# Three reorderings in a one-core diffusion layer: a gathered row inside the gate step, softmax normalising ahead of rotations, one engine per PSUM tile

## The chip, the cores and the metric

The kernel runs on one core of one Trainium2 chip. The metric is device microseconds (us) of one execution, here the median of three runs. One further execution was profiled; every view below comes from it. Engines are named as the profile names them: PE multiplies matrices, PEld loads its weights, DVE is the vector engine, ACT the scalar (activation) engine, POOL the general one, SP issues most transfers.

## The reference

One layer of a hybrid backbone over 512 latent tokens and 256 context tokens, width 1024. Modulated tokens go through one wide input projection into three branches: a gated linear recurrence, a convolution, and attention with 8 heads over 768 keys with a rotary position code. The branches are gated, summed, projected, and a first layer norm follows. Then come the product-key experts: each token picks 16 of 16384 single-neuron experts in each of 8 heads, and

    act = gelu(u_tab[expert] . t)        # 128 picked rows per token
    out = sum over k of (g * act)_k * v_tab[expert]_k

and a second layer norm.

## The kernel before, in words

The order of the work on PE, DVE, ACT and POOL is written out by hand: what stands first in the program goes first in that engine's queue. SP's transfers are not in that hand order; the framework plans them. All float32 products are made of three passes over a high part (ACT rounds, `whi`, `ph`, ...) and a low part (DVE subtracts the high part from the value, `wlo`, `pl`, ...): `mm3`, lines 142 to 144. So a low part always waits for ACT's high part.

**Attention** (`slot`, `norm`, `softmax`, `turn`) goes over 8 heads times 4 blocks of 128 queries. In slot n the kernel divides block n's exponentials by their sum (`norm`, L947 and L948), takes the row maximum of block n + 1 and starts its exponentials (`softmax`, L938 to L942), multiplies the scores of block n + 2 (`scores`), and transposes block n (`turn`: PE L956, then ACT and DVE split the result into `PTh` and `PTl`). Between these stand pieces of the next heads' projections, passed in as `early`, `mid` and `late`; among them the rotation of a query or key (`rope`, L831 to L833), whose first DVE operation waits for a PE product, and `fetch_next`, which splits the next weight block.

**Norm 1** (`project`, `normalise`, `turn1`, `modulate`, `parts1`) takes token blocks 1, 2, 3, 0. `turn1` transposes a normalised block into two PSUM tiles `pt` of four 128 x 128 pieces each; `modulate` scales and shifts the pieces into `tf`: for most blocks DVE takes the four of the first tile and ACT the four of the second; for block 3 DVE takes pieces 0 to 4 and ACT 5 to 7, so both read the second tile. `parts1` then splits `tf` into `xh` (ACT) and `xl` (DVE or POOL), which the first expert product `pu` reads.

**The expert loop.** Tokens 128 to 511 are not gathered: all 128 x 128 expert scores are computed densely. Pass i multiplies the gated activations of expert group i (`ph`, `pl`, 128 x 384) with 128 rows of the v table, `second`: 6 results, 18 matmuls of 512 columns into `acc`. Up to pass 69 the activations of group n = i + 1 were made earlier (they lie in `arun`, or come back from DRAM). From n = 71 on, pass i also makes them, `first`: 24 matmuls of 384 columns into `pa`. `weigh` multiplies the activations by the gates (L1602, DVE), and `halves` splits them: ACT makes `ph` (L137), DVE `pl` (L138). `ph` and `pl` have two buffers each, `wraw` (the landing place of weight blocks) three. The first 128 tokens are done by gathering: POOL fetches one row of the u or v table per token (L1478), 128 + 128 rows in all, into seven `raw` buffers, so up to six are asked for ahead; DVE multiplies each by the token and sums (L1489), or adds it to the running output (L1497). `shares` hands each pass its number of these `gather_step`s, about 1.18 up to pass 69 and 3.2 from there on (by the factors 1.1 and 3.0 in `budget`); they wait in the list `todo` and `some` takes them out between matmuls.

In DVE's queue a pass up to 69 therefore stands so: gate product, (ACT makes `ph`), `pl`, two `wlo`, one or two rows. From there on: two `wlo` of u, the rows, two `wlo` of v, gate product, (ACT makes `ph`), `pl`. In the last 32 passes `prepare` adds operations for the end: two small PE products, and in eight passes a DVE operation of 128 x 1024.

Of the kernel before, what the change touches and what calls it, by code (L numbers as in the profile page):

```python
# [9 lines left out]
F32 = mybir.dt.float32  # L10
# [7 lines left out]
AF = mybir.ActivationFunctionType  # L18
# [5 lines left out]
NB, NBC = T // 128, TC // 128  # L24
H = 8
# [69 lines left out]
def body(tc, I, O):  # L95
    nc = tc.nc
    V, A, P, G = nc.vector, nc.scalar, nc.tensor, nc.gpsimd
# [38 lines left out]
    def split(hi, lo, src):  # L136
        A.activation(hi, src, AF.Copy)  # L137
        V.tensor_sub(lo, src, hi.bitcast(F32))  # L138
# [12 lines left out]
    def pspow(out, ps, mul, tmp):  # L151

        V.tensor_scalar(tmp, ps, mul, EPS, op0=ALU.mult, op1=ALU.add)
        G.tensor_tensor(out, tmp, mhalf[:, :tmp.shape[-1]], op=ALU.pow)
# [79 lines left out]
    todo, ready = [], []  # L234
# [38 lines left out]
    for h in range(-1, H):  # L273
        n = h + 1
# [46 lines left out]
    def go(*gens):  # L321
        for g in gens:
            next(g, None)
# [94 lines left out]
    def query(h):  # L418
        x_ = hd[h]
        w = feed('in', Z_Q + h)  # L420
        ps = pmm.tile([128, T], F32, name="mm")
        yield from product(ps, w, xhl, 2)
        s = hp.tile([128, T], F32, name="sg")
        A.activation(s, ps, AF.Sigmoid)
        x_.q = hp.tile([128, T], F32, name="q", bufs=1)
        V.tensor_mul(x_.q, ps, s)
        yield
        x_.KM = hp.tile([128, T], F32, name="KM")
        V.tensor_add(x_.KM, x_.KS[:, 0, :], x_.KS[:, 1, :])
        x_.QP = hp.tile([128, 2, T], F32, name="QP")  # L430
        for d in range(2):
            V.tensor_mul(x_.QP[:, d, :], x_.q, x_.F[:, d, :])
        x_.tot = x_.F
        yield
# [128 lines left out]
    def norm():  # L563

        bc = pms.tile([128, T], F32, name="ms")
        P.matmul(bc, ones[:, 0:1].to_broadcast([128, 128]), usum, start=True, stop=True)
        qsum = hp.tile([128, T], F32, name="scT")
        last = None
        for j in range(KT):
            uj = u[:, j, :]  # L570
            V.scalar_tensor_tensor(uj, bc, -1.0 / D, uj, op0=ALU.mult, op1=ALU.add)
            sq = hp.tile([128, T], F32, name="KM")
            A.activation(sq, uj, AF.Square)
            if j:
                G.tensor_add(qsum, last, sq)
            last = qsum if j else sq
            if j % 3 == 2:
                yield
        yield
        st = pms.tile([128, NB], F32, name="ms")  # L580
        for b in range(NB):
            P.matmul(st[:, b:b + 1], qsum[:, b * 128:(b + 1) * 128], ones, start=True, stop=True)
        t1 = const.tile([128, NB], F32, name="lt")
        rs = const.tile([128, NB], F32, name="lrs")
        pspow(rs, st, 1.0 / D, t1)
        yield
        uhl.extend([mp.tile([128, KT, T], F32R, name="uhi"), hc.tile([128, KT, T], F32R, name="og")])
        bc = pst.tile([128, NB, 128], F32, name="bc")
        for b in range(NB):
            P.matmul(bc[:, b, :], rs[:, b:b + 1].to_broadcast([128, 128]), ident, start=True, stop=True)  # L590
        bc = bc[:].rearrange("p b t -> p (b t)")
        V.tensor_mul(u[:, 0, :], u[:, 0, :], bc)
        yield
        for j in range(KT):
            uj = u[:, j, :]
            if j + 1 < KT:
                V.tensor_mul(u[:, j + 1, :], u[:, j + 1, :], bc)
            s = mp.tile([128, T], F32, name="ms", bufs=2)
            A.activation(s, uj, AF.Sigmoid, scale=chan['clg'][:, j:j + 1], bias=chan['clb'][:, j:j + 1])
            V.tensor_scalar(uj, uj, chan['clg'][:, j:j + 1], chan['clb'][:, j:j + 1], op0=ALU.mult, op1=ALU.add)  # L600
            V.tensor_mul(uj, uj, s)
            A.activation(uhl[0][:, j, :], uj, AF.Copy)
            if j:
                V.tensor_sub(uhl[1][:, j - 1, :], u[:, j - 1, :], uhl[0][:, j - 1, :].bitcast(F32))
            yield
        V.tensor_sub(uhl[1][:, KT - 1, :], u[:, KT - 1, :], uhl[0][:, KT - 1, :].bitcast(F32))
        yield
# [48 lines left out]
    ip, f_, b_, q_ = inputs(0), direction(0, 0), direction(0, 1), query(0)  # L656
# [27 lines left out]
    for h in range(H):  # L684
        n = h + 1
# [7 lines left out]
        if n < H:  # L693
            ip, f_, b_, q_ = inputs(n), direction(n, 0), direction(n, 1), query(n)
# [70 lines left out]
    a_ = adas()  # L765
# [184 lines left out]
    def turn(b):  # L950
        p_ = pb.pop(b)[0]
        for q_ in range(2):
            pt = ppt.tile([128, 3, 128], F32, name="pt")
            for j in range(3):
                c = q_ * 3 + j
                P.transpose(pt[:, j, :], p_[:, c * 128:(c + 1) * 128], ident)  # L956
            o_ = [t_[:, q_ * 3:q_ * 3 + 3, b * 128:(b + 1) * 128] for t_ in PT]
            split(o_[0], o_[1], pt)
# [7 lines left out]
    def slot(n, early=(), late=(), mid=(), pre=()):  # L966

        h, b = divmod(n, NB)
        norm(h, b)
        if n + 1 < NB * H:  # L970
            softmax(*divmod(n + 1, NB))
        go(*pre)
        if n + 2 < NB * H:
            scores(*divmod(n + 2, NB))
        fetch_next()
        if b == 0 and h:
            out(h - 1)
        go(*early)
        fetch_next()
        go(*mid)  # L980
        turn(b)
        go(*late)
        fetch_next()

# [37 lines left out]
    for g in range(4):  # L1022
        n = 8 * g
# [139 lines left out]
    def modulate(b, pts):  # L1163
        tfs = []
        for q_, pt in enumerate(pts):
            tf = op.tile([128, 4, 128], F32, name="tf", bufs=4)
            for i in range(4):
                j = q_ * 4 + i
                if j > 4 if b == 3 else q_:
                    A.activation(tf[:, i, :], pt[:, i, :], AF.Identity, scale=gs[:, j:j + 1], bias=bs[:, j:j + 1])  # L1170
                else:
                    V.tensor_scalar(tf[:, i, :], pt[:, i, :], gs[:, j:j + 1], bs[:, j:j + 1], op0=ALU.mult, op1=ALU.add)
            tfs.append(tf)
        return tfs
# [70 lines left out]
    NA = 32  # L1245
# [9 lines left out]
    arun = gap.tile([128, NA, TD], F32, name="gt")  # L1255
# [335 lines left out]

    ph = {}

    def halves(i2, a_):
        names = ("raw", "raw") if i2 >= NT - 2 else ("ph", "pl")
        ph[i2] = [pp.tile([128, TD], F32R, name=n, bufs=RB[1] if n == "raw" else 2) for n in names]
        split(ph[i2][0], ph[i2][1], a_)

    def weigh(n, a_):

        v_ = a_.rearrange("p (b t) -> p b t", t=GB)
        V.tensor_tensor(v_, v_, gates[n // GN][:, :, n % GN, :], op=ALU.mult)  # L1602
        halves(n, a_)
        if n % GN == GN - 1:
            del gates[n // GN]
        read_gates(n)
# [16 lines left out]
    back = {}  # L1623
# [11 lines left out]
    todo = []  # L1635
# [6 lines left out]
    def first(n, left):  # L1642

        a_ = gap.tile([128, TD], F32, name="a", bufs=4)
        ps = pa.tile([128, TD], F32, name="pa")
        w = UV.pop(('u', n))
        for k in range(KT):
            mm3(ps, [t_[k // 4][:, k % 4, :] for t_ in w], [t_[:, k, :] for t_ in thd], k == 0, k == KT - 1)
            if k % 2:
                some(left - k // 2)  # L1650
        A.activation(a_, ps, AF.Gelu_apprx_tanh)
        return a_
# [69 lines left out]
    for i in range(NT - LAST):  # L1722
        n = i + 1
        todo += shares(i)
        left = 6
        if NU <= n:
            fetch(('u', n + 1))
            left = 10
            a_ = first(n, left)
        else:  # L1730
            if n + 1 == NU:
                fetch(('u', NU))
            if NA <= n + 1 < NU:
                back[n + 1] = gap.tile([128, TD], F32, name="a", bufs=4)
                nc.sync.dma_start(back[n + 1], ad[n + 1 - NA])
            weigh(n, arun[:, n, :] if n < NA else back.pop(n)[:])
        if ('v', n) not in UV:
            fetch(('v', n))
        for m in range(2):
            for b in range(NB - 1):  # L1740
                second(i, b, m)
                some(6 - 3 * m - b)
        if NU <= n:
            weigh(n, a_[:])
        if i >= NT - 32:
            prepare(i - NT + 32)
        if gathered[0] == 2 * NS_ and 0 not in nst:
            residual(0, 0)
            residual(0, 1)
            moments(0)  # L1750
            norm2(0, 0)
            norm2(0, 1)
        del UV['v', i], ph[i]
# [42 lines left out]
```

## Time and profile before

| | us |
|---|---|
| median of 3 runs | 2436.23 (2435.23 to 2440.38) |
| the profiled execution, its own time | 2440.56 |
| its span, first to last instruction | 2438.8 |
| PE busy | 2344.7 (96%) |
| DVE busy | 1935.6 (79%) |
| ACT busy | 1043.3 (43%) |
| POOL busy | 648.6 (27%) |
| mean granted TensorE clock | 0.99 of full speed |

Shares of busy time are means over stages: in some stages PE never stops, in others it waits for a low part. Attention runs from about 770 to 1037 us of the span, norm 1 until about 1155, the expert loop from 1603 to 2396.

### The profile page before, as it was taken

To read this page: it belongs to the slowest core of one execution; us is meant where nothing else is said; L and a number is where in the kernel's file an instruction comes from. 1 tells how busy PE (TensorE), PEld (TensorE's weight loads), DVE (VectorE), ACT (ScalarE), POOL (GpSimd) and SP (SyncE) were. 2 spreads that over 40 slices of the span, in tenths; PEclk is the share of its full clock that TensorE was granted. 3 is DMA by queue.
4 is the path that set the end of the run, shared out by engine and by line. 5 is a ranking of instruction groups with operands and counts; after the bars stand their busy time and mean duration, and the time that the engine had idled before them with its cause. 6 is when DMAs were issued, how large, how long until landed. Compare 5 with 4: busy or idle time off the path is not lost.

```text
span 2438.8 us, 34766 instructions
## 1 busy us (share of the span) xinstructions
PE 2344.7 (96%) x12547; PEld 2022.8 (83%) x12547; DVE 1935.6 (79%) x3736; ACT 1043.3 (43%) x2294; POOL 648.6 (27%) x555
## 2 busy tenths in 40 slices
PE   7999999999999999999999999999989999999997
PEld 3888888887887777877999999987767888898886
DVE  7788888887875566564999699968878788889886
ACT  5544444443423444643366645533333333332333
POOL 6000000002111000041688301122323344444432
PEclk9999999999999999999999999999999999999999
DMA  6211111111482111242323379999999989998962
GB/s 241 74 61 61 60 54 61 61 61 64 163 303 76 35 35 35 70 145 81 104 98 111 123 259 324 327 331 307 349 354 348 351 320 336 339 333 317 337 220 93
DMA packets 156973, 452.66 MB, mean 186 GB/s; under 512 B 16256, under 2 KB 60672, under 8 KB 154624
## 3 DMA queue, kind: packets, MB, share of 16 engines
q1 hardware_dynamic: 106976, 278.33, 32.9%
q0 software_dynamic: 36864, 134.23, 15.5%
q10 hardware_dynamic: 12960, 37.87, 4.1%
q8 instruction: 99, 1.62, 0.3%
q14 instruction: 74, 0.61, 0.1%
HBM read 411.77 MB, written 37.03 MB: 184 GB/s over the span
## 4 chain that ended last, share of the span: by engine, by line
PE 60%; DVE 24%; DMA 7%; ACT 5%; issue 3%; POOL 2%; ACTq 0%; DVEq 0%; POOLq 0%; SPq 0%
PE mm L142 13%; PE mm L144 13%; PE mm L143 13%; DVE wlo L131 6%; DVE raw L1489 4%; DMA wraw<-in_v_dram 3%; PE sc L455 2%; PE pg L1539 2%; ACT whi L129 2%; PE acc L142 2%; PE acc L143 2%; PE acc L144 2%; ACT ph L137 2%; DMA wraw<-in_uT_dram 2%; DVE ttok L1497 2%
## 5 line engine op out<-in xcount | busy, mean ns | idle before, releaser
L131 DVE TENSOR_TENSOR wlo<-wraw,whi 128x512 fp32r<-128x512 f32 x687 | 465.1, 719 | 156.3 <-ACT whi L129 155.0
L142 PE MATMUL mm<-xh,wlo 128*128 128x512 f32 (+1 forms) x1448 | 555.9, 384 | 12.4 <-POOL wlo L131 3.8
L143 PE MATMUL mm<-xl,whi 128*128 128x512 f32 (+1 forms) x1448 | 536.9, 371 | 2.1 <-DVE xl L1180 0.9
L144 PE MATMUL mm<-xh,whi 128*128 128x512 f32 (+1 forms) x1448 | 537.3, 371 | 0.0
L129 ACT ACTIVATE whi<-wraw 128x512 fp32r<-128x512 f32 x784 | 448.5, 621 | 98.7 <-DMA wraw<-in_v_dram 22.6
L142 PE MATMUL acc<-whi,pl 128*128 128x512 f32 x756 | 300.6, 398 | 24.1 <-DVE pl L138 17.2
L142 PEld LDWEIGHTS mm<-xh,wlo 128*128 128x128 f32 x1448 | 273.9, 189 | 46.0 <-POOL wlo L131 4.5
L144 PEld LDWEIGHTS mm<-xh,whi 128*128 128x128 f32 x1448 | 273.0, 189 | 37.1
L143 PEld LDWEIGHTS mm<-xl,whi 128*128 128x128 f32 x1448 | 273.9, 189 | 35.4 <-DVE xl L316 2.1
L143 PE MATMUL acc<-wlo,ph 128*128 128x512 f32 x756 | 301.5, 399 | 1.8 <-DVE wlo L131 0.7
L144 PE MATMUL acc<-whi,ph 128*128 128x512 f32 x756 | 297.5, 394 | 0.0
L1478 POOL DMA_INDIRECT raw<-in_u_dram,idx x128 | 146.9, 1148 | 470.2 <-DVE act L1489 411.1
L1478 POOL DMA_INDIRECT raw<-in_v_dram,idx x128 | 160.5, 1254 | 191.3 <-DVE ttok L1497 154.4
L142 PEld LDWEIGHTS acc<-whi,pl 128*128 128x128 f32 x756 | 143.2, 189 | 63.4 <-ACT whi L129 18.3
L137 ACT ACTIVATE ph<-a 128x384 fp32r<-128x384 f32 x94 | 49.4, 525 | 335.7 <-DVE a L1602 312.7
L550 DVE SCALAR_TENSOR_TENSOR u<-up,dw,u 128x512 f32<-128x512 f32 x240 | 179.5, 748 | 4.9
L143 PEld LDWEIGHTS acc<-wlo,ph 128*128 128x128 f32 x756 | 143.5, 190 | 42.9 <-DVE wlo L131 14.1
L144 PEld LDWEIGHTS acc<-whi,ph 128*128 128x128 f32 x756 | 143.5, 190 | 28.5
L1497 DVE SCALAR_TENSOR_TENSOR ttok<-raw,act,ttok 128x1024 f32<-128x1024 f32 x127 | 162.9, 1283 | 3.1
L142 PE MATMUL pa<-xh,wlo 128*128 128x384 f32 x456 | 155.3, 340 | 5.2 <-DVE wlo L131 5.2
L131 POOL TENSOR_TENSOR wlo<-wraw,whi 128x512 fp32r<-128x512 f32 x97 | 132.8, 1391 | 89.3 <-ACT whi L129 87.3
L144 PE MATMUL pa<-xh,whi 128*128 128x384 f32 x456 | 154.6, 339 | 0.0
(423 smaller groups left out, 4236.1 us busy)
## 6 DMA issues: line engine op xcount, KB each, us to landing
wraw<-in_uT_dram SPq DMA_DIRECT2D x128, 512.0 KB, 5.1
wraw<-in_v_dram SPq DMA_DIRECT2D x128, 512.0 KB, 5.8
wraw<-in_w_in_dram SPq DMA_DIRECT2D x96, 512.0 KB, 3.3
gd<-gs ACTq DMA_DIRECT2D x16, 1536.0 KB, 7.7
gr<-gd SPq DMA_DIRECT2D x60, 288.0 KB, 9.2
ohi<-in_w_adaT_dram SPq DMA_DIRECT2D x32, 512.0 KB, 5.4
wraw<-in_wq_dram SPq DMA_DIRECT2D x16, 512.0 KB, 3.3
ad<-a ACTq DMA_DIRECT2D x39, 192.0 KB, 4.7
```

The lines of the kernel that those rows point to most:

```text
L129: A.activation(hi, r, AF.Copy)
L131: subs[i].tensor_sub(lo, r, hi.bitcast(F32))
L137: A.activation(hi, src, AF.Copy)
L142: P.matmul(out, ll, rh, start=first, stop=False)
L143: P.matmul(out, lh, rl, start=False, stop=False)
L144: P.matmul(out, lh, rh, start=False, stop=last)
L455: P.matmul(x_.ps[:, b, :], x_.KM[:, b * 128:(b + 1) * 128], ap3(x_.QP, T + b * 128, [2 * w_, 64 // w_], [w_ - T, 2], [1, w_]), start=True, ...
L550: V.scalar_tensor_tensor(acc, up[:, i:i + T], dw[:, j, i:i + 1], acc, op0=ALU.mult, op1=ALU.add)
L1478: G.indirect_dma_start(out=r, out_offset=None, in_=I['u'] if n < NS_ else I['v'], in_offset=bass.IndirectOffsetOnAxis(ap=idx0[:, n % NS_:n ...
L1489: V.tensor_tensor_reduce(out=r, in0=r, in1=ttok, scale=1.0, scalar=0.0, op0=ALU.mult, op1=ALU.add, accum_out=act[:, s_:s_ + 1])
L1497: V.scalar_tensor_tensor(ysb, r, act[:, s_:s_ + 1], ysb, op0=ALU.mult, op1=ALU.add)
L1539: P.matmul(ps[:, i, :], o3[:, q_, :, i], o1[:, i, :], start=q_ == 0, stop=q_ == 1)
```

## The change

Three edits. In attention, block n + 1 is normalised in slot n, behind `turn(b)` and ahead of `late` and the last `fetch_next`, and no longer at the start of slot n + 1. In norm 1, block 3's pieces are shared out as the other blocks' are. In the loop, one `gather_step` taken from `todo` stands between ACT's `ph` and DVE's `pl`: up to pass 69 the first of the pass, from there on the last one, held back until `weigh`.

```diff
     def slot(n, early=(), late=(), mid=(), pre=()):
         h, b = divmod(n, NB)
-        norm(h, b)
+        if n == 0:
+            norm(h, b)
         if n + 1 < NB * H:
             softmax(*divmod(n + 1, NB))
...
         turn(b)
+        if n + 1 < NB * H:
+            norm(*divmod(n + 1, NB))
         go(*late)
         fetch_next()
...
-                if j > 4 if b == 3 else q_:
+                if q_:
                     A.activation(tf[:, i, :], pt[:, i, :], AF.Identity, scale=gs[:, j:j + 1], bias=bs[:, j:j + 1])
...
-    def halves(i2, a_):
+    def halves(i2, a_, between):
...
-        split(ph[i2][0], ph[i2][1], a_)
-
-    def weigh(n, a_):
+        hi, lo = ph[i2]
+        A.activation(hi, a_, AF.Copy)
+        between()
+        V.tensor_sub(lo, a_, hi.bitcast(F32))
+
+    def weigh(n, a_, between=lambda: None):
...
-        halves(n, a_)
+        halves(n, a_, between)
...
             left = 10
+            held = todo.pop() if todo else lambda: None
             a_ = first(n, left)
...
-            weigh(n, arun[:, n, :] if n < NA else back.pop(n)[:])
+            weigh(n, arun[:, n, :] if n < NA else back.pop(n)[:], todo.pop(0) if todo else lambda: None)
...
         if NU <= n:
-            weigh(n, a_[:])
+            weigh(n, a_[:], held)
```

## Rows read from the trace of the kernel before

**Rows 1.** Waits, 1600 to 1912 us: who waited for whom, us, times, longest.
```profile
DVE pl L138 <- ACT ph L137: 51.8, 70, 3.6
...
PE acc L142 <- DVE pl L138: 6.0, 11, 0.6
```
**Rows 2.** Timeline of DVE, 1808 to 1836 us: start, us, instruction, count [idle before].
```profile
1826.12 0.55 DVE L1602 TENSOR_TENSOR a<-a,gr 128x384 f32<-128x384 f32 x1
1827.40 0.56 DVE L138 TENSOR_TENSOR pl<-a,ph 128x384 fp32r<-128x384 f32 x1 [0.73 <-ACT ph L137]
...
1830.28 1.22 DVE L1489 CUSTOM_DVE_ANT_0 raw<-raw,ttok 128x1024 f32<-128x1024 f32 x1
...
1831.43 0.55 DVE L1602 TENSOR_TENSOR a<-a,gr 128x384 f32<-128x384 f32 x1
```
**Rows 3.** Timeline of PE, first matmul of two passes before pass 70.
```profile
1665.34 0.39 PE L142 MATMUL acc<-whi,pl 128*128 128x512 f32 x1
...
1669.42 0.39 PE L142 MATMUL acc<-whi,pl 128*128 128x512 f32 x1
```
**Rows 4.** Windows of the loop: busy us (count) per engine, clock, DMA share, GB/s.
```profile
1603.20:1738.50 135.30, 130.90 (x558) 102.99 (x559) 110.39 (x194) 49.04 (x93) 39.69 (x37) 1.00 0.93 321
1738.50:1802.40 63.90, 57.63 (x235) 44.07 (x234) 47.01 (x83) 20.93 (x39) 16.38 (x15) 0.97 1.03 383
1802.40:1916.20 113.80, 110.39 (x469) 85.82 (x469) 95.00 (x167) 40.63 (x78) 34.49 (x31) 1.00 0.96 344
1916.20:2161.10 244.90, 238.00 (x1178) 215.29 (x1177) 207.04 (x291) 87.93 (x171) 112.56 (x89) 0.98 0.93 338
2161.10:2395.60 234.50, 225.06 (x1109) 201.58 (x1108) 199.80 (x249) 83.16 (x163) 89.27 (x72) 0.98 0.80 282
```
**Rows 5.** Waits, 1912 to 2405 us.
```profile
DVE pl L138 <- ACT ph L137: 36.8, 56, 0.9
```
**Rows 6.** Timeline of DVE, passes from 70 on; the last row is `prepare`'s.
```profile
2074.46 0.59 DVE L1602 TENSOR_TENSOR a<-a,gr 128x384 f32<-128x384 f32 x1
...
2077.43 3.92 DVE L1497 SCALAR_TENSOR_TENSOR ttok<-raw,act,ttok 128x1024 f32<-128x1024 f32 x3
...
2082.48 0.58 DVE L1602 TENSOR_TENSOR a<-a,gr 128x384 f32<-128x384 f32 x1
...
2087.68 1.29 DVE L131 TENSOR_TENSOR wlo<-wraw,whi 128x512 fp32r<-128x512 f32 x2 [3.41 <-ACT whi L129]
...
2210.04 1.22 DVE L1679 TENSOR_TENSOR gt<-gt 128x1024 f32<-128x1024 f32 x1
```
**Rows 7.** Timeline of PE, first matmul of two passes after pass 70.
```profile
1989.01 0.33 PE L142 MATMUL pa<-xh,wlo 128*128 128x384 f32 x1
...
1997.32 0.33 PE L142 MATMUL pa<-xh,wlo 128*128 128x384 f32 x1
```
**Rows 8.** Gathered rows (tile raw), 1600 to 2360 us: issue to landing.
```profile
DMA to landing us min/median/max: 4.9/7.4/10.7
```
**Rows 9.** Timeline of DVE and PE in attention.
```profile
808.17 0.69 DVE L831 TENSOR_TENSOR asq<-mm,sinT 128x512 f32<-128x512 f32 x1 [2.38 <-PE mm L829]
810.29 0.62 DVE L948 TENSOR_SCALAR P<-P,ssum 128x768 f32<-128x768 f32 x1
812.67 0.50 PE L142 MATMUL mm<-xh,wlo 128*128 128x512 f32 x1 [0.77 <-DVE qT L873]
840.62 0.63 PE L956 MATMUL pt<-ident,P 128*128 128x128 f32 x4 [1.15 <-DVE P L948]
```
**Rows 10.** Timeline of norm 1, block 3.
```profile
1133.41 1.68 DVE L1172 TENSOR_SCALAR tf<-pt,gs,bs 128x128 f32<-128x128 f32 x5
1135.13 1.16 ACT L1170 ACTIVATE tf<-pt,bs,gs 128x128 f32<-128x128 f32 x3 [2.56 <-DVE tf L1172]
...
1136.85 0.69 PE L142 MATMUL pu<-xh,wlo 128*128 128x384 f32 x1 [3.21 <-ACT xh L1179]
```
**Rows 11.** Window just behind it: columns as in group 4.
```profile
1136.00:1142.80 6.80, 5.82 (x17) 5.45 (x18) 3.17 (x8) 2.84 (x5) 0.55 (x1) 0.50 0.19 77
```

## The prediction

> **What bounds the kernel now.** I read the page first: PE is busy 96% of the span, but "busy" holds modelled ends, so the question is where PE waits, and for whom. The sum of waits over the loop comes next: up to pass 69 DVE waits for ACT's high part in every pass, 51.8 us in 70 waits, and PE waits for `pl` in 11 [rows 1]. The timeline of DVE then shows that its queue has no other hole: from one gate product to the next, 1826.12 to 1831.43, it takes 5.31 us with two rows, one of which is 1831.43 - 1830.28 = 1.15 us, so 4.16 us with one row, 0.73 of it the wait for `ph` [rows 2]. PE needs less: an undisturbed pass is 1669.42 - 1665.34 = 4.08 us [rows 3]. With 1.18 rows to a pass DVE takes 4.16 + 0.18 x 1.15 = 4.37 us; the window from 1802.4 holds 469 / 18 = 26 passes in 113.8 us, 4.38 each [rows 4]. DVE, waiting included, sets the pace, not PE; the reader is to see that a PE at 97% is the one that waits.
>
> From pass 70 on the two are level. PE's undisturbed pass is 1997.32 - 1989.01 = 8.31 us [rows 7]. DVE's pass with three rows is 2082.48 - 2074.46 = 8.02 us [rows 6]; a row of this kind is 3.92 / 3 = 1.3 us [rows 6], so 3.2 rows make about 8.3, of which 36.8 / 56 = 0.66 is the wait for `ph` [rows 5]. A DVE that is level recovers nothing: what it loses once, to a late weight block or to `prepare`'s operation, reaches PE.
>
> The surplus of the loop over PE's own pace follows from the windows [rows 4]: 31 passes in 135.3 us (558 / 18; 31 x 4.08 = 126.5, surplus 8.8); 13 + 26 passes in 177.7 (159.1, surplus 18.6); 28 passes in 244.9 (1178 / 42; 232.7, surplus 12.2); 26 passes in 234.5 (216.1 and some 1.8 for `prepare`'s products, surplus 16.6). Together 56 us are there to be won at most. The half-clock stretches behind the longer waits are in them (mean clock 0.97 to 0.98).
>
> **The row inside the split.** Nothing is added: the same rows are taken from the same list, each pass's number is unchanged, and no transfer changes. The moved row is DVE's (with a one-column read behind a u row), and it frees one buffer, so that POOL's next fetch is issued up to one `pl` and two `wlo` earlier. It stands in the 0.73 us (later 0.66) in which DVE waited. Behind it in DVE's queue stand `pl`, the `wlo` pair and the next gate product; PE's 18 matmuls wait for `pl`. The row outlasts `ph` by 1.15 - 0.73 = 0.42 us, so `pl` comes later behind its own gate product, but that product itself comes one row earlier. DVE's pass shrinks to 4.37 - 0.73 = 3.64 us, below PE's 4.08, and later to 8.3 - 0.66 = 7.64, below 8.31. What is late next is PE itself, or the transfers.
>
> Window by window:
> - 31 passes: surplus 8.8. DMA share 0.93 leaves room; I keep 2.2 for transfers that are late as now (estimate) and take -6.6 (bounds 0 and -8.8).
> - 39 passes: 63.9 x 383 + 113.8 x 344 = 63.6 MB must move in them. At the 383 GB/s of the first of the two windows, the highest rate here, that is 166 us against 177.7 now. PE's 159.1 is out of reach; I take -8, nearer to the 166 than to no gain (bounds 0 and -11.7).
> - 28 passes: surplus 12.2. Most of it is two or three late weight blocks, such as the 3.41 us for which DVE stood at 2087.68 [rows 6]. The DVE gains 0.67 us of lead in each pass (8.31 - 7.64), so after five or six passes such a wait stays on DVE and does not reach PE. The earliest ones come before the lead is built: -5 (bounds 0 and -12.2).
> - 26 passes: surplus 16.6. `prepare`'s eight operations of 1.22 us [rows 6] against a new slack of 0.67 in each pass and the lead: nearly gone. The work for the gathered tokens' norm near the end remains in part: -11 (bounds -5 and -16.6).
> - A faster loop moves the same bytes in less time; I allow one more wait of the size of that 3.41: +3.
>
> Loop: -6.6 - 8 - 5 - 11 + 3 = -27.6 us.
>
> A rule of the Trainium skill speaks against the second of these terms. The rows show 383 GB/s over 64 us and 358 as the mean of the 39 passes (63.6 MB in 177.7 us) [rows 4]. "DMA: Bandwidth & Descriptors", section "Where 436 GB/s comes from", holds that transfers between HBM and SBUF are bound at about 358 GB/s per core. By that page these passes would be at their bound already, and the sum would be 8 us less of a gain; the trace, which ran 64 us above that figure, does not agree.
>
> **Normalising ahead of the rotations.** Per slot the same two DVE operations, some 0.77 us by start-to-start times (0.62 and a small one ahead), change their place. In the three slots where a key is rotated late, DVE stood idle 2.38 us before the rotation, and the normalising came behind it, ahead of a row maximum and the key's scaling for which PE then waited 0.77 us at 812.67 [rows 9]. The normalising now fits into the 2.38 and PE gains 0.77 three times (the same steps come back at 874.66 and 936.73): -2.3. Where `late` holds a value's split or a `fetch_next`, these come 0.77 later; PE's wait of 1.15 at 840.62 [rows 9], which follows from ACT and DVE and recurs three times, covers that, so I cost it at nothing. Without that cover it would be +0.77 three times; bounds of the edit: -4 and +1.
>
> **One engine per PSUM tile.** For block 3 ACT waits 2.56 us until DVE's fifth piece is done at 1135.09, then does three in 1.16 us; the first `xh` follows and PE starts `pu` at 1136.85 after 3.21 us of waiting [rows 10]. After the change ACT starts with the end of the transposes, 1136.85 - 3.21 = 1133.64, and does four in 4 x 0.39 = 1.55: 1135.2 instead of 1136.29. DVE's four are done at about 1134.8, so ACT decides: -1.1. Then PE ran 6.8 us at a granted clock of 0.50, the 1.2 GHz level [rows 11]. A shorter wait may bring a shorter stretch at that level; the 6.8 us hold at most 3.4 us of loss. I take -0.9 (bounds 0 and -3.4). Together -2.0.
>
> **Sum.** -27.6 - 2.3 - 2.0 = -32 us against the profiled execution's own 2440.56: 2408.6. That execution was 4.3 us above the median of the runs, so against the median 2436.23 it is 2404; I say 2405.
>
> **Rivals.**
> *The transfers hold the loop.* For it: share 0.93 to 1.03 in four of five windows [rows 4], and a weight block's split waited 3.41 us for its data. Against it: the share counts 383 GB/s as 1.03, and 28 passes need 82.8 MB in 233 us, 355. Then the 39 and the 28 passes give nothing and the last 26 half of their 11: -6.6 - 5.5 = -12, with the other edits -16: 2420. Chance 0.22.
> *The edit in the loop does not do what it says:* DVE stops waiting for `ph` and waits as long for `whi`, which ACT makes behind `ph`. For it: one queue on ACT makes both, and 3.41 us of such a wait stand in the trace [rows 6]. Against it: in the old order `wlo` followed 0.56 us behind the start of `pl` [rows 2] with no wait in the timeline, and now `whi` has 0.42 us more. Only the -4.3 of the two small edits stay: 2432. Chance 0.09.
> *Slower: rows that land late hold `pl`.* In the old place a late row held nothing of its own pass; now `pl`, the weights' low parts and PE's 18 or 42 matmuls stand behind it. It decides as soon as a row takes longer to land than DVE takes for the six ahead of it: from pass 70 on 6 / 3.2 x 8.31 = 15.6 us. Now the longest landing is 10.7 [rows 8]. If a fuller queue made rows 1.3 us late in one of three of the last 93 passes, that would cost 31 x 1.3 = 40 us against the 32 gained: 2444. Chance 0.05.
>
> **How the numbers follow.** The forecast has 0.64; its own range is 2393 to 2418. Slow end: the second window's 8 and one more 3.4 are lost, 2416, and 2 for the clock in norm 1. Fast end: the four bounds, 49, less 10 for transfers are 39 in place of 27.6: 2393.5. The range of eight in ten, 2390 to 2427, takes in the first rival and leaves out the second and third. 0.2% is 4.9 us, about what a measurement can tell from no change. Forecast and first rival are faster by more: 0.86. The second is within it: 0.09. Slower: 0.05.
>
> **What would show it.** In the loop, DVE's wait for `ph` must shrink from 51.8 and 36.8 us to nearly nothing, passes of 4.1 to 4.2 us must stand in the first and third window, and PE's waits for `pl` must go. If DVE's waits for `whi` or the waits for `wraw` grow instead, the first or second rival holds; a DVE that waits for a gathered row shows the third. In attention the wait at 812.67 must go in all three places; in norm 1 ACT's 2.56. The forecast is wrong if PE's passes stay at 4.38 us although DVE is no longer occupied. SP's order is planned, not written: if the transfers are issued in another order, late blocks may fall elsewhere.

## The result, and the profile after

The changed kernel takes 2396.73 us, median of 4 runs (2394.18 to 2399.99), against 2437.07 for the kernel before in the same comparison: ratio 0.9834, 95% interval 0.9816 to 0.9852, so 1.7% faster, some 40 us. The forecast was 2405 in a range of 2390 to 2427: the sign and the mechanism held, the gain was 8 us larger than said. The two profiled executions are 41.9 us apart (2440.56 and 2398.68).

The page after: the span, the busy times, and the shares of the engines in the chain that ended last; below them the same shares before.

```profile
span 2396.9 us, 34804 instructions
...
PE 2324.3 (97%) x12547; PEld 2021.3 (84%) x12547; DVE 1926.6 (80%) x3735; ACT 1045.3 (44%) x2295; POOL 641.4 (27%) x555
...
PE 77%; DVE 13%; DMA 5%; ACT 2%; issue 2%; POOL 1%; ACTq 0%; SPq 0%; DVEq 0%; POOLq 0%
```
```profile
PE 60%; DVE 24%; DMA 7%; ACT 5%; issue 3%; POOL 2%; ACTq 0%; DVEq 0%; POOLq 0%; SPq 0%
```

The chain passed from DVE to PE. PE's busy time fell by 20 us with the same 12547 matmuls: its busy share, 96% before and 97% now, is no measure of what is left to win.

The windows of the loop, cut at the same passes as [rows 4], the second and third of which are one here: us, busy (count) of PE, PEld, DVE, ACT, POOL, clock, DMA share, GB/s.

```profile
1597.80:1727.80 130.00, 128.43 (x558) 104.55 (x559) 111.78 (x198) 49.13 (x93) 36.64 (x38) 1.00 0.96 341
1727.80:1895.30 167.50, 162.23 (x704) 132.63 (x703) 139.75 (x249) 63.35 (x119) 45.34 (x46) 0.99 1.02 381
1895.30:2129.00 233.70, 232.82 (x1177) 211.70 (x1176) 196.81 (x283) 85.25 (x165) 111.36 (x87) 1.00 0.95 348
2129.00:2353.70 224.70, 220.08 (x1109) 199.38 (x1108) 198.77 (x252) 85.79 (x167) 91.38 (x72) 0.99 0.81 296
```

Against [rows 4] the four parts are 5.3, 10.2, 11.2 and 9.8 us shorter: 36.5 of the 41.9. Attention gave 2.3, norm 1 3.4, and two half-clock stretches elsewhere (one more near 609 us, ahead of attention, and one fewer near 1347) go with +1.9 and -1.6.

DVE's waits up to pass 69, and from there on, which answer to [rows 1, 5] (us, times, longest):

```profile
DVE wlo L131 <- ACT whi L129: 26.0, 12, 5.8
DVE pl L1603 <- ACT ph L1601: 20.3, 37, 0.7
...
DVE wlo L131 <- ACT whi L129: 58.9, 31, 7.6
DVE pl L1603 <- ACT ph L1601: 2.6, 4, 0.7
```

The wait for `ph` fell from 51.8 to 20.3 us and from 36.8 to 2.6. What is left, and the growth of the waits for `whi` (14.6 and 33.2 us before), are a different thing, as one pass shows. DVE, ACT and PE, a pass up to 69:

```profile
1828.93 1.22 DVE L1492 CUSTOM_DVE_ANT_0 raw<-raw,ttok 128x1024 f32<-128x1024 f32 x1
...
1830.81 0.56 DVE L1603 TENSOR_TENSOR pl<-a,ph 128x384 fp32r<-128x384 f32 x1 [0.65 <-ACT ph L1601]
...
1830.25 0.53 ACT L1601 ACTIVATE ph<-a 128x384 fp32r<-128x384 f32 x1 [2.51 <-PE acc L144]
...
1834.08 0.39 PE L142 MATMUL acc<-whi,pl 128*128 128x512 f32 x1
...
1838.16 0.39 PE L142 MATMUL acc<-whi,pl 128*128 128x512 f32 x1
```

The row stands ahead of `pl`, and DVE waits 0.65 us all the same, because ACT's `ph` itself waited 2.51 us for PE to let go of one of the two `ph` buffers. `pl` ends at 1831.37 and PE takes it up at 1834.08: DVE is 2.7 us ahead. In the pass of [rows 2] it was 0.5 us ahead: `pl` ended at 1827.96, and this matmul read it first:

```profile
1828.48 0.39 PE L142 MATMUL acc<-whi,pl 128*128 128x512 f32 x1
```

A wait for the engine that sets the pace costs nothing; the sign to read is PE's own pass, 1838.16 - 1834.08 = 4.08 us. From pass 70 on the same is seen with `whi`: DVE and ACT.

```profile
1968.30 1.29 DVE L131 TENSOR_TENSOR wlo<-wraw,whi 128x512 fp32r<-128x512 f32 x2 [1.44 <-ACT whi L129]
...
1967.26 0.49 ACT L1657 ACTIVATE a<-pa 128x384 f32<-128x384 f32 x1 [3.84 <-PE pa L144]
```

ACT, which makes `whi` next, stands behind its activation out of `pa`, and that waits for PE. PE's waits in the loop were 17.2 us for `pl`, 6.3 for `whi` and 5.2 for `wlo` before; after:

```profile
PE acc L142 <- ACT whi L129: 5.6, 4, 4.3
PE acc L142 <- DVE pl L1603: 5.0, 3, 2.3
PE acc L143 <- DVE wlo L131: 1.1, 5, 0.2
PE acc L142 <- issue: 0.6, 1, 0.6
PE pa L142 <- DVE wlo L131: 0.5, 1, 0.5
```

### The profile page after: what moved, and what is told of

It reads as the page before. It is cut to its first block, busy times and chain, and to the rows that moved or that the text cites. A ratio compares the mean times of both kernels' runs of the same rounds, so it can differ in the third digit from the quotient of the medians.

```text
span 2396.9 us, 34804 instructions
## 1 busy us (share of the span) xinstructions
PE 2324.3 (97%) x12547; PEld 2021.3 (84%) x12547; DVE 1926.6 (80%) x3735; ACT 1045.3 (44%) x2295; POOL 641.4 (27%) x555
## 4 chain that ended last, share of the span: by engine, by line
PE 77%; DVE 13%; DMA 5%; ACT 2%; issue 2%; POOL 1%; ACTq 0%; SPq 0%; DVEq 0%; POOLq 0%
PE mm L142 13%; PE mm L144 13%; PE mm L143 13%; PE acc L143 6%; PE acc L144 6%; PE acc L142 6%; PE pa L142 3%; PE pa L144 3%; PE pa L143 3%; PE sc L455 2%; PE pg L1542 2%; DMA wraw<-in_v_dram 2%; DMA wraw<-in_uT_dram 1%; DVE wlo L131 1%; DVE eb L1346 1%
## 5 line engine op out<-in xcount | busy, mean ns | idle before, releaser
L1481 POOL DMA_INDIRECT raw<-in_u_dram,idx x128 | 137.1, 1071 | 456.4 <-DVE act L1492 393.3
L1492 DVE CUSTOM_DVE_ANT_0 raw<-raw,ttok 128x1024 f32<-128x1024 f32 x128 | 155.1, 1218 | 0.0
```

The source lines that it names most:

```text
L1481: G.indirect_dma_start(out=r, out_offset=None, in_=I['u'] if n < NS_ else I['v'], in_offset=bass.IndirectOffsetOnAxis(ap=idx0[:, n % NS_:n ...
L1492: V.tensor_tensor_reduce(out=r, in0=r, in1=ttok, scale=1.0, scalar=0.0, op0=ALU.mult, op1=ALU.add, accum_out=act[:, s_:s_ + 1])
```

## The experiments

All lengths of the loop's parts in one table: us between PE's first product (`acc`) of passes 0, 31, 70, 98 and 124, from the timeline of each run's profiled execution. A part can differ by 4 us between executions of the same code (before and no_loop have one and the same loop). Each ratio is to runs of the kernel before on the same chip.

| run | median us | ratio to before, interval | 0-30 | 31-69 | 70-97 | 98-123 |
|---|---|---|---|---|---|---|
| before | 2437.07 | | 135.3 | 181.9 | 245.7 | 242.3 |
| changed | 2396.73 | 0.9834 (0.9816-0.9852) | 130.0 | 171.6 | 236.6 | 230.4 |
| no_loop | 2431.96 | 0.9988 (0.9975-1.0001) | 133.2 | 182.4 | 242.0 | 242.6 |
| loop_only | 2399.75 | 0.9846 (0.9829-0.9863) | 130.2 | 172.0 | 235.0 | 228.8 |
| row_ahead | 2428.65 | 0.9970 (0.9958-0.9983) | 136.2 | 180.8 | 235.6 | 240.2 |
| loop_early | 2415.34 | 0.9902 (0.9866-0.9937) | 129.5 | 170.9 | 245.7 | 245.7 |
| loop_late | 2416.88 | 0.9916 (0.9888-0.9943) | 134.6 | 181.2 | 238.0 | 231.3 |
| dve_short | 2402.10 | 0.9856 (0.9829-0.9883) | 129.6 | 173.5 | 235.8 | 234.7 |
| dve_long | 2414.99 | 0.9910 (0.9883-0.9937) | 133.4 | 176.9 | 233.5 | 235.3 |
| after_again | 2396.35 | 0.9835 (0.9819-0.9851) | 129.9 | 171.7 | 233.5 | 230.3 |
| loads_spread | 2392.77 | 0.9820 (0.9799-0.9842) | 130.9 | 164.9 | 233.5 | 233.1 |
| lead3 | 2393.15 | 0.9819 (0.9805-0.9834) | 129.8 | 170.3 | 235.7 | 229.8 |
| spread_attn | 2391.68 | 0.9814 (0.9799-0.9830) | 130.5 | 164.6 | 238.2 | 228.9 |
| all_three | 2388.81 | 0.9804 (0.9790-0.9819) | 130.5 | 163.3 | 233.5 | 230.3 |

**no_loop and loop_only: the parts by themselves.** Each undoes the other's edits, as in the change's diff.

> The changed kernel without its edit in the loop: only the normalising ahead of the rotations and the PSUM tile per engine stay. Theory (the loop's edit is worth 36 us, the two small ones what the two traces show for attention and norm 1, -2.3 and -3.4): 2431 to 2433 against 2437, and 1.2 in ten for no change that can be measured. Rival (the small edits shift the loop's transfers and so carry part of the loop's gain): 2425 or less, with fewer waits in the loop than before.

> The loop's edit alone: attention and norm 1 as in the kernel before. Theory: 2401, 4 to 6 us above the changed kernel; passes of 4.08 and 8.31 us as in the changed kernel. Rival (the loop's gain needs the earlier start that the small edits give): 2410 or more.

Both rivals are out. The two small edits are worth 4.8 us against the 2436.74 of before on that chip, the loop's edit 37.0; they add up to 41.8 where the whole gave 40.3. The 4.8 alone are not clear of no change, since the interval reaches 1.0001. loop_only came 3 us above the changed kernel, a little nearer than said. The loop needs no help from an earlier start.

**row_ahead: the same row, one place earlier.** It leaves the wait empty, but frees the row's buffer even earlier.

```diff
     def weigh(n, a_, between=lambda: None):
 
+        between()
         v_ = a_.rearrange("p (b t) -> p b t", t=GB)
         V.tensor_tensor(v_, v_, gates[n // GN][:, :, n % GN, :], op=ALU.mult)
-        halves(n, a_, between)
+        halves(n, a_, lambda: None)
```

> As the changed kernel, but the row stands ahead of the gate product, not between the high and the low part: the same rows in the same passes, the same buffers freed one row early, the same transfers, and the wait for the high part is left empty. Theory (the gain is the filled wait of 0.73 and 0.66 us): the wait for the high part comes back with about 50 and 37 us, passes of 4.3 to 4.4 us, and the time is 2428 to 2435. Rival (the gain comes from row buffers that are freed earlier and so from earlier transfers): 2397 to 2405.

DVE's waits of this kernel, up to pass 69 and from there on:

```profile
DVE pl L1603 <- ACT ph L1601: 47.5, 68, 0.7
...
DVE pl L1603 <- ACT ph L1601: 37.8, 57, 0.9
```

The wait is back nearly in full and the gain is gone: 3.3 us against no_loop are left, and the two intervals overlap. Up to pass 69 nothing is left of it: 317.0 us in the first two parts against 315.6. So it is the filled wait, not the buffer that comes free earlier. From pass 70 on 475.8 stand against 484.6. That pair of traces says more than the medians do, for the traced execution of row_ahead is the shortest of its ten (2424.71); whether the row's place late in the pass gives something there without filling a wait stays open.

**loop_early and loop_late: half the loop each.**

```diff
-            held = todo.pop() if todo else lambda: None
+            held = lambda: None                          # loop_early
...
-            weigh(n, arun[:, n, :] ..., todo.pop(0) if todo else lambda: None)
+            weigh(n, arun[:, n, :] ...)                  # loop_late
```

> The changed kernel, with the row between high and low part only up to pass 69; from pass 70 on the rows stand where they stood before. Theory (the parts of the loop add up as the two traces show them, 5.3 + 10.3 us up to pass 69 and 21.0 behind it): 2416 to 2419, passes of 4.08 us up to pass 69, and from there DVE's waits for the high part as before, about 37 us. The lead of 2.7 us that DVE has at pass 69 is kept and still takes the first late block of the last part, the 3.2 us wait of PE near pass 74. Rival (the rows ahead set the later part too): 2410 or less.

> The changed kernel, with the row between high and low part only from pass 70 on. Theory: passes of about 4.38 us up to pass 69, a lead of DVE of 0.6 us at pass 70 in place of 2.7, so the first late block, near pass 74, reaches PE with 1 to 3 us as in the kernel before, and the rest of the gain from there on stays: 2411 to 2415. Rival (as the prediction had it, the last part is worth 16 and not 21): 2417 or more.

loop_early came a little below its expectation (runs from 2409.65 to 2421.72). Its first late block behind pass 70 cost PE 0.77 us near pass 74, where before it was 3.23: the lead was carried over. But later blocks then cost 2.9 and 3.0 us, and the part was no shorter in the traced execution, which is the longest of the four. loop_late missed its expectation by 2 us and reached the rival's edge: PE met the first late block with 2.31 us, the two last parts together were 469.3 us. These are PE's waits for that block, before, in loop_early and in loop_late:

```profile
1952.85 0.69 PE L142 MATMUL pa<-xh,wlo 128*128 128x384 f32 x1 [3.23 <-DVE wlo L131]
```
```profile
1932.36 0.50 PE L142 MATMUL acc<-whi,pl 128*128 128x512 f32 x1 [0.77 <-DVE pl L1603]
```
```profile
1946.97 0.44 PE L142 MATMUL pa<-xh,wlo 128*128 128x384 f32 x1 [2.31 <-DVE wlo L131]
```

Three kernels without any edit there (before, no_loop, loop_early) have 484.6 to 491.4, three with the edit in the whole loop (changed, loop_only, after_again) 463.8 to 467.0: some 23 us, of which the lead from the first half is worth about 4 (469.3 against their mean of 464.9). The 4 rest on one trace, and executions of the same code can differ by as much; the waits above are the better evidence for the lead.

**dve_short and dve_long: how much DVE has to spare.** One more operation in each pass, of 512 or of 1024 columns.

```diff
         between()
+        for _ in range(1):
+            V.tensor_scalar(ysb[:, :1024], ysb[:, :1024], 1.0, None, op0=ALU.mult)
         V.tensor_sub(lo, a_, hi.bitcast(F32))
```

> The changed kernel with one more operation of DVE in every pass of the loop, between the row and the low part: a multiplication by 1.0 of 512 columns of the gathered tokens' sum, 0.42 us by the rows of its kind. Theory (DVE has 0.44 us to spare in a pass up to 69 and 0.67 behind): PE keeps its 4.08 and 8.31 us, and only the lead that takes up late blocks builds more slowly: 2397 to 2403. Rival (DVE still sets the pace in the changed kernel): 0.42 us in each of some 124 passes, about 2449.

> As the one before with 1024 columns, about 0.82 us, more than DVE has to spare. Theory: (0.82 - 0.44) x 70 + (0.82 - 0.67) x 54 = 27 + 8 = 35 us more, 2432, passes of 4.46 and 8.46 us. Rival (DVE sets the pace already): 0.82 x 124 = 102 us more, 2498. If DVE has more to spare than the sum of its rows says: 2410 or less.

The short one lasts 0.427 us; 123 of them, 52.5 us of work, cost 5 us: DVE no longer sets the pace. For the long one the group of its instructions, and two `pl` with one row and the new operation between them, say why it costs 18 us and not 35:

```profile
L1604 DVE TENSOR_SCALAR ttok<-ttok 128x1024 f32<-128x1024 f32 x122 | 84.6, 694 | 4.1
...
1849.53 0.55 DVE L1605 TENSOR_TENSOR pl<-a,ph 128x384 fp32r<-128x384 f32 x1
...
1852.93 0.69 DVE L1604 TENSOR_SCALAR ttok<-ttok 128x1024 f32<-128x1024 f32 x1
1853.54 0.55 DVE L1605 TENSOR_TENSOR pl<-a,ph 128x384 fp32r<-128x384 f32 x1
```

The operation is 0.69 us, not the 0.82 that was estimated from shorter ones. With it the prediction's slack gives (0.69 - 0.44) x 70 + (0.69 - 0.67) x 54 = 18.6 us, and 18.5 were measured by the ratios; but that agreement is luck, since both slacks were too small. Where DVE waits for nothing, a pass of the changed kernel takes it 3.29 us with one row (lead3 below shows two such passes) and 7.09 with three behind pass 70 (lines in the account of the prediction). With 1.18 and 3.2 rows that is 3.5 and 7.35 us, so 0.58 and 0.96 to spare. The new operation makes the first 1853.54 - 1849.53 = 4.01, 0.72 more: (0.72 - 0.58) x 70 = 10 us up to pass 69, where 8.7 came, and from pass 70 on, by the same sum, nothing, since 0.72 is less than 0.96; 1.8 came. The traced execution is 12.0 us longer than the changed kernel's and the shortest of dve_long's four, 4.3 us under their median; where the rest of the 18 lies is not shown.

**lead3: what holds the lead.** Three buffers for `ph` and `pl`.

> The changed kernel with three buffers in place of two for the high and for the low part. Its trace shows DVE's lead on PE standing at 2.7 us up to pass 69 and at 3.6 us behind it, as if held there. Theory (the two buffers hold it): the lead grows by a pass, to about 6.8 us and more, PE's waits of 4.27 us at 1779 and of 1.9 us at 2136 are taken up: 2388 to 2392. Rival (ACT, the weight blocks or the rows hold the lead, not the buffers): it stays below 4 us, and the time at 2394 to 2399.

ACT's waits up to pass 69 in the changed kernel, and in this one:

```profile
ACT ph L1601 <- PE acc L144: 118.4, 49, 2.6
ACT whi L129 <- DMA wraw<-in_v_dram: 23.8, 12, 6.0
```
```profile
ACT ph L1601 <- DVE a L1608: 63.5, 35, 2.9
...
ACT whi L129 <- DMA wraw<-in_v_dram: 51.5, 21, 5.4
...
ACT ph L1601 <- PE acc L144: 13.7, 6, 2.5
```

Up to pass 69 the theory holds. ACT no longer waits for PE, and DVE runs ahead at its own pace until the third buffer stops it; one such `pl` and the first matmul that reads it:

```profile
1718.49 0.55 DVE L1603 TENSOR_TENSOR pl<-gt,ph 128x384 fp32r<-128x384 f32 x1
...
1721.78 0.55 DVE L1603 TENSOR_TENSOR pl<-gt,ph 128x384 fp32r<-128x384 f32 x1
...
1725.60 0.56 DVE L1603 TENSOR_TENSOR pl<-a,ph 128x384 fp32r<-128x384 f32 x1 [0.46 <-ACT ph L1601]
...
1732.95 0.39 PE L142 MATMUL acc<-whi,pl 128*128 128x512 f32 x1
```

DVE's pass is 3.29 us, and the lead 1732.95 - 1726.16 = 6.8 us. But then the transfers come in: ACT waits 51.5 us for weight blocks in place of 23.8, and PE still waits 2.67 us at 1776. From pass 70 on the lead stays at 3.64 us as in the changed kernel: there PE's `pa` product holds it, as the 3.84 us of ACT's wait showed, and the theory was wrong there. 2393.15 lies between the two expectations, and its interval overlaps that of after_again.

**loads_spread: 4 MB that come too early.** In the changed kernel SP issues `prepare`'s eight loads of 512 KB in passes 31 to 41, as soon as `arun` is free, though the first of them is needed in pass 100. Here ACT issues them, later: the queue and the time change together.

```diff
+    LOADS = [(9, 'ln1_g'), (10, 'ln1_b'), (3, 0), ...]
...
+    def load(j, n):
...
+        nc.scalar.dma_start(fin[j], rowbc(I[n], D) if isinstance(n, str) else x1d[n])
...
-                nc.sync.dma_start(fin[j], rowbc(I[n], D))
...
-                nc.sync.dma_start(xb, x1d[(k - 3) // 2])
...
+        if NU <= i and (i - NU) % 4 == 1 and LOADS:
+            load(*LOADS.pop(0))
```

> The changed kernel with the eight loads of 512 KB for the last blocks (norm gains, biases and residual rows) issued by ACT, one in every fourth pass from pass 72 on, where SP issues them all around pass 32 to 38. Theory (these 4 MB in the stretch with the fullest queues are what makes the weight blocks there late): the waits of 0.55 and 4.27 us at 1753 and 1779 go, and with them the half-clock stretch behind: 2389 to 2391, against 2397. Rival (the queues are full there with or without them, and later passes get what the earlier are spared): 2395 to 2402.

DMA between 1735 and 1790 us, in the changed kernel and in this one:

```profile
DMA packets 8933, 21.72 MB, mean 395 GB/s; under 512 B 825, under 2 KB 4665, under 8 KB 8930
```
```profile
DMA packets 8356, 19.66 MB, mean 357 GB/s; under 512 B 767, under 2 KB 4607, under 8 KB 8353
```

The stretch was full and is no longer; 13 weight blocks are issued in it instead of 11, the waits of 0.55 and 4.27 us shrink to one of 0.80, and the part 31 to 69 goes from 171.6 to 164.9. By the medians it is 4 us, 2 less than the theory had, and the intervals overlap. Against after_again the other parts gave 3.8 of 6.8 us back, against the changed kernel's trace 0.5 of 6.7: how much is kept is not settled. That the queues are full with or without these loads, the rival's reason, is refuted by the part's length.

**spread_attn, all_three and after_again.** after_again is the changed kernel once more. The other two have the loads of loads_spread. In the first the normalising also goes back behind `late` where that holds a value's split (`if v_ in late`); in the second the third buffers are added.

> The changed kernel once more, as the base for the three others: 2394 to 2399.

> The kernel with the eight loads on ACT's queue, and in attention the normalising goes back behind the slot's late work in those slots where that work is a value's split. In the changed kernel PE waits 0.93 us for that split three times. Theory (the prediction's cover: the next wait, 1.16 us some 7 us later, ends at the same time with or without the first): the three waits of 0.93 go, the three behind them grow, attention keeps its length within 0.5 us, and the time stays at that of the kernel with the spread loads, 2390 to 2394. Rival (nothing covers them): attention 2.8 us shorter, 2388 to 2390.

> Third buffers, spread loads and the attention edit of the run before together. Theory (the longer lead and the spread loads take up the same waits, so they don't add up in full): 2385 to 2390. Rival (without effect of the buffers): 2390 to 2394.

PE's waits in attention, in the changed kernel and in spread_attn:

```profile
813.80 0.50 PE L142 MATMUL mm<-xh,wlo 128*128 128x512 f32 x1 [0.78 <-DVE qT L873]
...
834.30 0.44 PE L897 MATMUL mm<-ident,zg 128*128 128x128 f32 x2 [0.93 <-DVE vl L138]
...
841.75 0.85 PE L956 MATMUL pt<-ident,P 128*128 128x128 f32 x6 [1.16 <-DVE P L948]
```
```profile
813.33 0.50 PE L142 MATMUL mm<-xh,wlo 128*128 128x512 f32 x1 [0.78 <-DVE qT L873]
...
835.21 0.87 PE L956 MATMUL pt<-ident,P 128*128 128x128 f32 x6 [0.26 <-DVE P L948]
...
841.32 0.85 PE L956 MATMUL pt<-ident,P 128*128 128x128 f32 x6 [1.18 <-DVE P L948]
```

The three waits of some 0.93 us shrink to 0.2 and nothing is won: from 813.80 to 841.75 it was 27.95 us, from 813.33 to 841.32 it is 27.99, and attention as a whole stays at 306.9. The wait in front of `P` ends when DVE gets there, however long PE has stood before. all_three is the fastest version here, 2388.81 us, on the same chip as after_again with 2396.35; PE's pace leaves little more in the loop (its waits there are 5.6 us).

## Why the prediction was right, step by step

*The bound.* Right: DVE with its waits set the pace, and with one wait filled PE does, at 4.08 and 8.31 us [rows 3, 7]. no_loop, row_ahead and dve_short show it from three sides. DVE's own pass became shorter than said: 3.5 and 7.35 us, not 3.64 and 7.64.

*31 and 39 passes.* -6.6 - 8 = -14.6 was said; -5.3 - 10.2 = -15.5 came in the pair of traces, -14.4 as the mean of three kernels without the edit there (before, no_loop, loop_late) against three with it (changed, loop_only, after_again). The sum is nearer than its terms. The second term rested on 383 GB/s as the most that these transfers reach: the part ran at 381 over 167.5 us. Its bound was the bytes of that part, though, and loads_spread shows that 4 MB of them were not needed there.

The Trainium skill's bound of about 358 GB/s for a core, cited ahead, would have kept these passes where they were; they ran above it. The Trainium skill's page "HBM Reference", section "Specifications (TRN2)", says that a core streaming alone measures well above that share. This trace, of one core, agrees in that it ran above it: 381 GB/s over these passes, 395 between 1735 and 1790 us.

*28 and 26 passes, and the late block.* -5 - 11 + 3 = -13 was said; -21.0 came, and some -23 in the three against three. These are the terms that were mis-sized: the surplus of 28.8 us from [rows 4] was counted rightly, but nearly three quarters of it and not half were to be had. The step that failed is that a late block's wait stays on DVE only "after five or six passes" of 0.67 us, and that "the earliest ones come before the lead is built". The lead was there at pass 70: from pass 9 on DVE stood, but for late blocks and passes with two rows, at the 2.7 us that two buffers allow. And it comes back sooner. After the late block of pass 90 in the changed kernel, `pl` of passes 90, 91 and 92, and the first matmul that reads the first and the last of them:

```profile
2065.82 0.55 DVE L1603 TENSOR_TENSOR pl<-a,ph 128x384 fp32r<-128x384 f32 x1
...
2072.91 0.55 DVE L1603 TENSOR_TENSOR pl<-a,ph 128x384 fp32r<-128x384 f32 x1
...
2080.01 0.55 DVE L1603 TENSOR_TENSOR pl<-a,ph 128x384 fp32r<-128x384 f32 x1
```
```profile
2066.74 0.39 PE L142 MATMUL acc<-whi,pl 128*128 128x512 f32 x1
...
2083.35 0.39 PE L142 MATMUL acc<-whi,pl 128*128 128x512 f32 x1
```

DVE's pass with three rows is 2072.91 - 2065.82 = 7.09 us, where it was 8.02 [rows 6]: filling the wait of 0.66 took 0.93 off. The lead goes from 2066.74 - 2066.37 = 0.37 to 2083.35 - 2080.56 = 2.79 us, 1.2 a pass, and in the third pass it is at its 3.64 again. Why the filled wait is worth more than its length was not tried. The late block allowed for at +3 did not come: the rate rose from 338 to 348 GB/s in the 28 passes and PE's waits there fell from 3.2, 0.4 and 3.3 us to one of 0.9. Five half-clock stretches of the 54 passes before became one after. Against the mean of the three kernels without the edit there, loop_late, which lacked the lead at pass 70, gained 18.7 us in these parts, and the three with the whole edit 23.1. So beside the allowance of 3, about 4 us are the lead at pass 70; for the 2.7 above the 16 that were said, the quicker lead is the likely reason, but no run shows it by itself.

*Attention.* -2.3 was said, -2.26 came (between PE's waits at 775.20 and 1084.38 before, 309.18 us, and at 777.09 and 1084.01 after, 306.92). The sign named for it was wrong: the wait of 0.77 at 812.67 [rows 9] still stands as 0.78. The rotation it waits for did come 0.76 us earlier, counted from the start of attention, but so did PE, which no longer waits 0.54 for `P` ahead of it. The cover that was claimed for the value's split held, as spread_attn shows. That the size is the edit's, two other traces say: both executions above have a half-clock stretch near 788; loop_only and row_ahead, without and with the edit, have none there and took 307.57 and 305.43 us, 2.14 apart.

*Norm 1.* ACT and DVE: -1.1 said, -1.08 came (1084.38 to 1136.85 before, 1084.01 to 1135.40 after); ACT's wait of 2.56 us fell to 1.12, and its four pieces took 1.50. The clock: -0.9 said, -2.3 came (1136.85 to 1151.74 before, 1135.40 to 1147.95 after), as the stretch at half clock of [rows 11] was missing altogether. That is partly luck: loop_only, which lacks the edit, took 14.11 us there (1137.26 to 1151.37), and so did three executions that have it (last section). What the edit brings to the clock is not measured by this pair.

*The rivals.* The transfers do not hold the loop as a whole; they held it around 1750 to 1790 us. The sign chosen for the second rival, longer waits for `whi`, appeared (47.8 us became 84.9) without its effect: DVE was ahead of PE when it waited. No wait of DVE for a gathered row stands in the loop.

## What to carry to other kernels

Filling a short wait in every pass of the engine that sets the pace pays until the next engine sets it: here 66 us of DVE's waits for `ph` went and the loop became 36.5 us shorter. The engine that is now ahead builds a lead that takes up late transfers; measure how fast it builds from a pass in which that engine waits for nothing, count it from the first pass on, and find what caps it (buffers, or a product of the bottleneck itself). After such a change, waits of that engine may grow: read the bottleneck's own pass, not the other's waits. A short wait of the bottleneck that goes away is worth nothing where its next wait ends at a time that other work sets.

## What the runs showed of the hardware

The half clock is not settled here by the length of the wait ahead of it. In all 12 executions with norm 1's edit PE waits some 2.1 us at this place; in 9 the granted clock stayed at 1.00 (2.4 GHz) there, in 3 (row_ahead, loop_late, dve_long) a stretch at 0.50 (1.2 GHz) followed. The window just behind the wait in the changed kernel and in row_ahead:

```profile
1135.40:1142.20 6.80, 6.43 (x35) 6.20 (x36) 3.15 (x8) 1.99 (x3) 0.55 (x1) 1.00 0.19 77
```
```profile
1134.30:1141.10 6.80, 6.40 (x26) 6.18 (x27) 3.17 (x8) 2.01 (x3) 0.55 (x1) 0.75 0.19 77
```

In the same time 26 matmuls began in place of 35, and the way from `pu` to the wait for `xl` behind it took 14.1 us in place of 12.55. So a term for the clock can be bounded from rows, as it was, but not placed inside the bounds from one execution.
